# Decay rows on GpSimd's queue, a later convolution of B and C, and pooled-mixing weights split two groups at a time

## The chip, the cores and the metric

The kernel runs on one core of one Trainium2 chip. The time is device microseconds of one launch, from the first instruction to the last, and the time of a kernel is the median of its runs. Engines are named as the profile names them: PE is TensorE (matmuls; PEld its loads of weights), DVE is VectorE, ACT ScalarE, POOL GpSimd and SP SyncE. SyncE does no arithmetic here, it issues transfers. A transfer (DMA) stands in the queue of the engine that issues it, and an engine that waits before an issue holds back all issues behind it.

## The reference, cut to what matters

One layer of a hybrid trunk for 512 tokens of width 1024, in float32. A normed and modulated input `h` goes through one large projection, whose columns are split over three mixers that work beside each other. Their outputs are projected, gated and summed; an MLP follows.

```python
z, xbc, dt_raw, q, k, v, u, gates = jnp.split(h @ w_in, splits, axis=-1)

xbc = silu(causal_dwconv(xbc, conv_w, conv_b))          # 4 taps, 1536 channels
xs, Bm, Cm = jnp.split(xbc, [1024, 1280], axis=-1)      # x; B and C: 2 groups x 128 each
dt = softplus(dt_raw + dt_bias)                         # 16 heads
# _ssd, chunks of 128 tokens:
X = xc * dt
a_cum = cumsum(dt * A)                                  # within a chunk
decay = exp(where(causal, a_cum[l] - a_cum[s], -inf))   # per head, 128 x 128
y_diag = ((C @ B^T) * decay) @ X
y_off = (C @ prev) * exp(a_cum)                         # prev: states carried over chunks
y = y_diag + y_off + D * xc;  y = rms(y * silu(z)) * ssd_norm_w;  y_ssd = y @ w_ssd_out

# three groups of dilated attention, 4 heads of 128 each, mixed by their log-sum-exp
y_attn = sum_g(softmax_g(lse) * out_g) @ w_attn_out

# pooling: windows 2, 4, 8, 16, one per group of 256 channels
pooled = window_mean(u_g) - u_g
y_pool = (concat_g(pooled_g @ w_pool_mix[g]) * pool_scale) @ w_pool_out

x = x + g1 * ((g_ssd * y_ssd + g_attn * y_attn + g_pool * y_pool) @ w_out)
x = x + g2 * (square(relu(h2 @ w_ff1)) @ w_ff2)         # h2: normed again, modulated
```

The modulation (shifts, scales and the gates g1, g2) is `silu(c) @ w_ada + b_ada`.

## The kernel before, in words

Everything lies transposed in SBUF, 128 channels on the partitions by 512 tokens, in blocks of that size; `blk` hands out 49 blocks in turn, `psm` and `acc` the 8 PSUM banks. A block that is handed out again is written only when its last reader is done; a load into it waits for that reader.

A float32 product is made of three products of halves: a weight tile `raw` (512 KB, 128x1024, issued on SP, L287) is split by ScalarE into a high part `wh` (cast, L279) and by VectorE into the rest `wl` (subtraction, L280), and `mm3` (L294, L295, L296) multiplies low by high, high by high, high by low. There are four buffers for `raw` and three pairs for the halves. `gemm_feat` makes four banks `psacc` of 512 tokens at once; `evac` copies them out. The modulation that is not yet needed is worked out along the way: `ada_load` (L240, two loads `wa` of 256 KB on SP) and `ada_dot` (L246, a product with a sum on VectorE, then `modv`), one such job at every second weight tile.

The program text is one long list of gemms; `tick()` is called after each weight tile and runs the next job of the list `side`, so that scores, convolutions, the state-space steps and the pooling lie between the matmuls of a gemm. Within the text a scheduler of the framework sets each engine's order by priority: loads and splits of weights are drawn ahead (AHEAD), evacuations too (SOON), the rest stands where it is written.

The stretch that the change touches runs from the values of the attention to the gates of the state-space branch:

- `attn_out` (L715 to L738), as side jobs of the gemm of B and C: TensorE sums one head's output in the bank `pso`, ScalarE copies it (L736), VectorE subtracts (L737).
- `conv_silu` (L846 to L852) for one tile of 128 channels: ScalarE scales (L848), VectorE adds three shifted taps (L850), ScalarE takes the silu (L852). It is called for B and C (four tiles, L1083) and for x (four tiles per group).
- `ssd_states`: the transposes of B, the product of B and C (`pscb`, L869; masked into `cb`, L870), then per chunk the transposes of x (`psX`), `X` (VectorE, L882), `Xd` (L887), the states `psst` (L891) and the carried states `prev` (first by ScalarE, L895, then by VectorE).
- `ssd_heads`: two heads at a time. The cumulated decay of each head stands as one row of 512 numbers in `prow`, a small tensor in DRAM. For each of the 16 heads one transfer spreads its row over 128 partitions into a block `M` (256 KB, L912, on SP). Then `e` (exp, ScalarE, L917), the differences (VectorE L924 for one head of a pair, ScalarE L922 for the other), the exp (ScalarE, L925), the product with `cb` (VectorE, L926), and the matmuls `psy` with `X` (L932).
- `project` (L751 multiplies by the gate `sg`), first for the attention.
- `pool` (windows by doubling shifted sums, VectorE) and `pool_mix` (L989 on): per group of channels a weight `wmix` of 128x512 is loaded (L991) and split by `wsplit`, in the same buffers as streamed weights, just ahead of its 12 matmuls into two banks `psmix`.

ScalarE keeps one table of functions at a time; a change from copies and exps to silu and back shows in the profile as `ACT_TABLE_LOAD`.

Of the kernel before, what the change touches and what calls it, by code (L numbers as in the profile page):

```python
# [10 lines left out]
F32 = mybir.dt.float32  # L11
F32R = mybir.dt.float32r
AF = mybir.ActivationFunctionType
ALU = mybir.AluOpType
# [3 lines left out]
P = 128  # L18
D = 1024
T = 512  # L20
# [78 lines left out]
def kernel(ctx: ExitStack, tc: tile.TileContext, a: dict, out: bass.AP, dbg=None):  # L99
    nc = tc.nc  # L100
# [3 lines left out]
    raws = ctx.enter_context(tc.tile_pool(name="raws", bufs=4))  # L104
    wsp = ctx.enter_context(tc.tile_pool(name="wsp", bufs=3))
    exp = ctx.enter_context(tc.tile_pool(name="exp", bufs=1))
# [6 lines left out]
    def uid(s):  # L113
        cnt[0] += 1
        return f"{s}_{cnt[0]}"

    class Slots:
# [12 lines left out]
        def free(self, t):  # L130
            self.idle.append(self.used.pop(id(t))[0])
# [3 lines left out]
    def blk(name, dt=F32):  # L135
        return sb.take(name, dt)
# [7 lines left out]
    def doubles(name, tags=("L0", "L1", "N0", "N1")):  # L144

        ts = [exp.tile([P, 2, T], F32R, tag=tag, name=uid(name)) for tag in tags]
        return [t[:, i, :] for t in ts for i in range(2)]

    def small(shape, name, bufs=1, dt=F32):
        return sm.tile(shape, dt, tag=name, name=uid(name), bufs=bufs)  # L150

    def psm(name="m"):
        return banks.take("ps" + name, F32)
# [9 lines left out]
    V, S = nc.vector, nc.scalar  # L163
# [112 lines left out]
    def wsplit(raw, shape):  # L276
        wh = wsp.tile(shape, F32R, tag="wh", name=uid("wh"))
        wl = wsp.tile(shape, F32R, tag="wl", name=uid("wl"))
        S.copy(wh, raw)  # L279
        V.tensor_tensor(wl, raw, wh.bitcast(F32), ALU.subtract)  # L280
        return wh, wl
# [59 lines left out]
    with tc.manual_schedule(engines={E.DVE, E.Activation, E.PE, E.SP}):  # L341
# [107 lines left out]
        var, rt, r, t = (small([P, 4], "rx" + n) for n in "vryt")  # L449
# [266 lines left out]
    def attn_out(h, pTs, vals):  # L716
        hs = slice(h * P, (h + 1) * P)
        op = psm("o")
        ov = op.rearrange("p (j r) -> p r j", r=4)
        for gi in range(3):  # L720
            pT, vs = pTs[gi], vals[gi]
            for b in range(4):
                if gi == 0:
                    od = op[:, b * P : (b + 1) * P]
                    for kb in range(max(0, b - 1), b + 1):
                        cs = (b % 2) * 2 * P + (kb - b + 1) * P
                        mm(od, lhsT=vs[kb][:, hs], rhs=pT[b // 2][:, cs : cs + P], start=(b == 0), stop=False, skip_group_check=True)  # L727
                else:
                    mm(ov[:, b, :], lhsT=vs[b][:, hs], rhs=pT[0][:, b * P : (b + 1) * P], start=False, stop=(gi == 2 and b == 3), skip_group_check=True)  # L729
            free(*pT)  # L730
        if h == 0:
            places = doubles("o")
            oh.extend(places[:4])
            ol.extend(places[4:])
        with tc.high_priority(offset=SOON):
            S.copy(oh[h], op)  # L736
            V.tensor_tensor(ol[h], op, oh[h].bitcast(F32), ALU.subtract)  # L737
        free(op)  # L738


# [29 lines left out]
    st = {}  # L770
# [75 lines left out]
    def conv_silu(x, n):  # L846
        t = blk("conv")
        S.activation(t, x, AF.Identity, bias=vc("conv_b", n), scale=cw[:, 3, n : n + 1])  # L848
        for i in range(1, 4):
            V.scalar_tensor_tensor(t[:, i:], x[:, : T - i], cw[:, 3 - i, n : n + 1], t[:, i:], ALU.mult, ALU.add)  # L850
        free(x)
        S.activation(t, t, AF.Silu)  # L852
        return t

    hp = lambda t: t.rearrange("p (h e) -> p h e", h=8)

    def ssd_states(g, xs, BC):

        BT, CT = BC[g], BC[2 + g]
        Bt, cb = blk("Bt"), blk("cb")  # L860
# [43 lines left out]
    def ssd_heads(g, j, xs, z):  # L904

        X, prev, cb, CT = st[g]
        pc, npc, prow = st["pc"], st["npc"], st["prow"]

        Ms = [blk("M") for _ in range(2)]
        for half in range(2):  # L910
            hd = g * 8 + 2 * j + half
            nc.sync.dma_start(Ms[half], prow[hd : hd + 1, :].broadcast_to([P, T]))  # L912
        yield
        e = blk("e")
        for half in range(2):
            hd, M, fs = g * 8 + 2 * j + half, Ms[half], slice(64 * half, 64 * half + 64)
            S.activation(e[fs, P:], M[fs, P:], AF.Exp, scale=-1.0)  # L917
            for c in range(4):
                cs = slice(c * P, (c + 1) * P)
                hc = slice(c * 16 + hd, c * 16 + hd + 1)  # L920
                if half:
                    S.activation(M[:, cs], M[:, cs], AF.Relu, bias=npc[:, hc])  # L922
                else:
                    V.tensor_scalar(M[:, cs], M[:, cs], pc[:, hc], 0.0, ALU.subtract, ALU.max)  # L924
            S.activation(M, M, AF.Exp, scale=-1.0)  # L925
            V.tensor_tensor(M, M, cb, ALU.mult)  # L926
        yield
        yp = psm("y")
        for c in range(4):
            cs = slice(c * P, (c + 1) * P)  # L930
            for half in range(2):
                mm(yp[half * 64 : half * 64 + 64, cs], lhsT=X[c][:, (2 * j + half) * 64 : (2 * j + half + 1) * 64], rhs=Ms[half][:, cs], start=True, stop=True)  # L932
        free(*Ms)
        y = xs[j]
        V.scalar_tensor_tensor(y, xs[j], dcol[:, 4 * g + j : 4 * g + j + 1], yp, ALU.mult, ALU.add)
        free(yp)
        op = psm("yo")
        for c in range(3):
            cs = slice((c + 1) * P, (c + 2) * P)
            mm(op[:, cs], lhsT=prev[c][:, j * P : (j + 1) * P], rhs=CT[:, cs], start=True, stop=True)  # L940
        V.tensor_tensor(e[:, P:], op[:, P:], e[:, P:], ALU.mult)
        free(op)
        V.tensor_tensor(y[:, P:], y[:, P:], e[:, P:], ALU.add)
        show(f"y{g}{j}", y)
        free(e)
        V.tensor_tensor(y, y, z[j], ALU.mult)
        free(z[j])
        if j == 3:
            free(*X, *prev, cb, CT)
        st["sums", g] = add_square(st.get(("sums", g)), y)  # L950
# [17 lines left out]
    def pool(half):  # L968
        us = evac(gemm_feat(w_in, 8, U + half, hh, hl), "u")
        for j in range(4):  # L970
            gi = 2 * half + j // 2
            u = us[j]
            cur, d = u, 1
            while d < WINDOWS[gi]:
                nx = blk("win")
                V.tensor_copy(nx[:, :d], cur[:, :d])
                V.tensor_tensor(nx[:, d:], cur[:, d:], cur[:, : T - d], ALU.add)
                if cur is not u:
                    free(cur)
                cur, d = nx, 2 * d  # L980
            V.tensor_tensor(cur[:, : d - 1], cur[:, : d - 1], C("edge")[:, gi * 16 : gi * 16 + d - 1], ALU.mult)
            V.scalar_tensor_tensor(cur, cur, 1.0 / d, u, ALU.mult, ALU.subtract)
            free(u)
            x, y = split(cur, "pd")
            free(cur)
            dh.append(x)
            dl.append(y)

    def pool_mix(gi):  # L989
        raw = raws.tile([P, 2, 256], F32, tag="raw", name=uid("wmix"))  # L990
        nc.sync.dma_start(raw, a["w_pool_mix"][gi])  # L991
        wh, wl = wsplit(raw, [P, 2, 256])
        for m in range(2):
            ps = psm("mix")
            cs = slice(m * P, (m + 1) * P)
            for k in range(2):
                mm3(ps, wh[:, k, cs], wl[:, k, cs], dh[2 * gi + k], dl[2 * gi + k], k == 0, k == 1)
            x, y = blk("poolh", F32R), blk("pooll", F32R)
            S.activation(x, ps, AF.Copy, scale=vc("pool_scale", gi * 2 + m))
            V.scalar_tensor_tensor(y, ps, vc("pool_scale", gi * 2 + m), x.bitcast(F32), ALU.mult, ALU.subtract)  # L1000
            free(ps)
            ph_.append(x)
            pl_.append(y)
        free(*dh[2 * gi : 2 * gi + 2], *dl[2 * gi : 2 * gi + 2])
# [12 lines left out]
    def call(f, *args):  # L1017
        side.append(lambda: f(*args))

    probs, vals, stats, pTs, oh, ol = [], [], [], [], [], []  # L1020
# [59 lines left out]
    for h in range(4):  # L1080
        call(out_head, h)
    ps = evac(gemm_feat(w_in, 8, BCC, hh, hl), "xc")
    BC = [conv_silu(ps[i], 8 + i) for i in range(4)]  # L1083
    xs0 = take_x(0)
    rest(1)
    do(ssd_states(0, xs0, BC), 6)
    z0 = take_z(0)
    do_heads(0, xs0, z0)
    xs1 = take_x(1)
    z1 = take_z(1)  # L1090
    do(ssd_states(1, xs1, BC), 6)
    sg = gate(GA, 0)
# [3 lines left out]
    project(a["w_attn_out"], 4, 1, oh, ol, sg, first=True)  # L1096
    show("oT", [h.bitcast(F32) for h in oh + ol])
    for half in range(2):
        pool(half)
        rest(2)  # L1100
        call(pool_mix, 2 * half)
        call(pool_mix, 2 * half + 1)
# [50 lines left out]
    with tc.manual_schedule(engines={E.DVE, E.Activation, E.PE}):  # L1153
# [64 lines left out]
        ps = out_block(tb, 0)  # L1218
        r = scale(sum_tokens(ta, sq))
        residual(tb, 0, ps)  # L1220
        ps = out_block(tb, 1)
# [262 lines left out]
```

## Time and profile before

| | us |
|---|---|
| three runs | 1097.83, 1096.16, 1095.39 |
| median | 1096.16 |
| the profiled execution | 1098.25 |
| its span | 1096.5 |
| PE busy | 1087.1 (99%) |
| DVE busy | 717.4 (65%) |
| ACT busy | 527.8 (48%) |
| POOL busy | 3.6 (0%) |
| six loads on GpSimd's queue (`al` four times, `toNat`, `toMod`) | 256 KB each |
| 16 loads of decay rows on SP's queue | 256 KB each |

The clock of TensorE was granted in full throughout (1.00). In the profile a time is counted from the start of the span, and a row of a timeline shows the start, the duration, the engine, the line, the operation, the tile written and the tiles read, and in brackets how long the engine sat idle before it and what released it. "psacc<-hl,wh" is a matmul that reads `hl` and `wh` and writes the bank `psacc`. A busy share near 100% of TensorE says that it nearly always had work, and the few stalls are found one by one, in the waits and in the starts of neighbouring matmuls. An idle time of VectorE or ScalarE matters only where TensorE then waits.

### The profile page before, as it was taken

What the parts mean: (1) busy time and instruction counts of PE and PEld (TensorE: products, weight loads), DVE (VectorE), ACT (ScalarE), POOL (GpSimd) and SP (SyncE); (2) the same over time, 40 slices, a digit from 0 to 9 for tenths busy, and PEclk for the clock granted to TensorE, in tenths of its full rate; (3) what the DMA queues carried; (4) which work ended last, traced back from release to release, by engine and by line L of the source; (5) the groups of instructions that cost most, each with busy time, mean ns of one, the idle gap of its engine ahead of it and who ended that gap; (6) DMA issues with size and microseconds to landing.
All of it is one profiled execution on the core that took longest, in us unless ns stands there. A gap on an engine that the chain in (4) does not pass through costs nothing.

```text
span 1096.5 us, 14976 instructions
## 1 busy us (share of the span) xinstructions
PE 1087.1 (99%) x5806; PEld 927.0 (85%) x5806; DVE 717.4 (65%) x1383; ACT 527.8 (48%) x845; POOL 3.6 (0%) x10
## 2 busy tenths in 40 slices
PE   9999999999999999999999999999999999999998
PEld 7878888888887877888888888899889989989987
DVE  8975874582776778568843424577787587686664
ACT  8965875543695536625432123354344334335330
POOL 0000000000000000000000000000000000000000
PEclk9999999999999999999999999999999999999999
DMA  9853342443542354321232325360214224134032
GB/s 349 306 183 98 128 134 86 152 168 102 173 125 87 117 181 136 104 97 58 96 115 97 106 96 163 97 230 1 79 57 154 65 90 136 59 114 135 20 116 77
DMA packets 46666, 133.98 MB, mean 122 GB/s; under 512 B 5362, under 2 KB 6130, under 8 KB 46596
## 3 DMA queue, kind: packets, MB, share of 16 engines
q1 hardware_dynamic: 45392, 130.28, 36.0%
q0 software_dynamic: 480, 1.57, 0.5%
q10 hardware_dynamic: 724, 1.18, 0.3%
q8 instruction: 45, 0.74, 0.3%
q14 instruction: 25, 0.20, 0.1%
HBM read 130.89 MB, written 2.13 MB: 121 GB/s over the span
## 4 chain that ended last, share of the span: by engine, by line
PE 87%; ACT 4%; DVE 3%; DMA 3%; issue 1%; SPq 0%; ACTq 0%; DVEq 0%
PE psacc L294 22%; PE psacc L296 22%; PE psacc L295 22%; PE psacc L1345 11%; PE psacc L534 4%; DMA M<-prow 2%; PE psS L613 1%; DMA wa<-in_w_ada_dram 1%; DVE conv L850 1%; ACT wh L279 1%; PE pso L729 1%; PE pso L727 1%; DVE wl L280 1%; PE pskT L597 0%; PE psqT L592 0%
## 5 line engine op out<-in xcount | busy, mean ns | idle before, releaser
L280 DVE TENSOR_TENSOR wl<-raw,wh 128x1024 fp32r<-128x1024 f32 x140 | 171.0, 1222 | 192.2 <-ACT wh L279 190.9
L279 ACT CAST wh<-raw 128x1024 fp32r<-128x1024 f32 x140 | 146.8, 1050 | 241.1 <-PE psacc L295 168.8
L294 PE MATMUL psacc<-hl,wh 128*128 128x512 f32 x416 | 166.6, 401 | 3.4 <-DVE X L882 2.2
L295 PE MATMUL psacc<-hh,wh 128*128 128x512 f32 x416 | 162.1, 390 | 0.0
L296 PE MATMUL psacc<-hh,wl 128*128 128x512 f32 x416 | 162.0, 390 | 0.0
L295 PE MATMUL psacc<-ah,wh 128*128 128x512 f32 (+1 forms) x260 | 100.4, 386 | 0.0
L294 PE MATMUL psacc<-al,wh 128*128 128x512 f32 (+1 forms) x260 | 100.4, 386 | 0.0
L296 PE MATMUL psacc<-ah,wl 128*128 128x512 f32 (+1 forms) x260 | 100.3, 386 | 0.0
L294 PEld LDWEIGHTS psacc<-hl,wh 128*128 128x128 f32 x416 | 78.2, 188 | 21.7 <-DVE X L882 2.7
L295 PEld LDWEIGHTS psacc<-hh,wh 128*128 128x128 f32 x416 | 78.2, 188 | 16.9 <-issue 1.4
L296 PEld LDWEIGHTS psacc<-hh,wl 128*128 128x128 f32 x416 | 78.1, 188 | 16.7
L294 PE MATMUL psacc<-wl,rh 128*128 128x512 f32 x192 | 76.9, 401 | 0.0
L296 PE MATMUL psacc<-wh,rl 128*128 128x512 f32 x192 | 75.5, 393 | 0.0
L295 PE MATMUL psacc<-wh,rh 128*128 128x512 f32 x192 | 75.3, 392 | 0.0
L296 PEld LDWEIGHTS psacc<-ah,wl 128*128 128x128 f32 x260 | 48.8, 188 | 9.9
L294 PEld LDWEIGHTS psacc<-al,wh 128*128 128x128 f32 x260 | 48.9, 188 | 9.7
L295 PEld LDWEIGHTS psacc<-ah,wh 128*128 128x128 f32 x260 | 48.9, 188 | 9.6
L1405 DVE SCALAR_TENSOR_TENSOR xr<-psacc,modv,xr 128x512 f32<-128x512 f32 (+1 forms) x65 | 44.7, 739 | 18.6 <-PE psacc L296 18.6
L246 DVE SCALAR_TENSOR_TENSOR wa<-wa,crow 128x512 f32<-128x512 f32 x64 | 43.1, 688 | 20.0 <-DMA wa<-in_w_ada_dram 20.0
L296 PEld LDWEIGHTS psacc<-wh,rl 128*128 128x128 f32 x192 | 36.0, 188 | 7.6
L294 PEld LDWEIGHTS psacc<-wl,rh 128*128 128x128 f32 x192 | 36.1, 188 | 7.3 <-ACT qT L593 0.2
L295 PEld LDWEIGHTS psacc<-wh,rh 128*128 128x128 f32 x192 | 36.1, 188 | 7.0
(408 smaller groups left out, 2360.8 us busy)
## 6 DMA issues: line engine op xcount, KB each, us to landing
raw<-in_w_in_dram SPq DMA_DIRECT2D x80, 512.0 KB, 3.5
raw<-in_w_ff_dram SPq DMA_DIRECT2D x52, 512.0 KB, 3.7
wa<-in_w_ada_dram SPq DMA_DIRECT2D x64, 256.0 KB, 3.6
wada<-in_w_ada_dram SPq DMA_DIRECT2D x14, 512.0 KB, 7.8
rawl<-in_w_ff_dram SPq DMA_DIRECT2D x12, 512.0 KB, 3.5
wst<-in_w_in_dram SPq DMA_DIRECT2D x16, 256.0 KB, 7.8
M<-prow SPq DMA_DIRECT2D x16, 256.0 KB, 3.8
raw<-in_w_ssd_out_dram SPq DMA_DIRECT2D x8, 512.0 KB, 3.5
```

What stands on the lines that cost most here:

```text
L246: V.scalar_tensor_tensor(wa[i], wa[i], 1.0, crow[i], ALU.mult, ALU.mult, accum_out=d[:, i : i + 1])
L279: S.copy(wh, raw)
L280: V.tensor_tensor(wl, raw, wh.bitcast(F32), ALU.subtract)
L294: mm(ps, lhsT=wh, rhs=xl, start=first, stop=False)
L295: mm(ps, lhsT=wh, rhs=xh, start=False, stop=False)
L296: mm(ps, lhsT=wl, rhs=xh, start=False, stop=last)
L534: mm(ps[j], lhsT=t[:, j, :], rhs=w, start=first, stop=last)
L613: mm(so[b], lhsT=qT[:, b * P : (b + 1) * P], rhs=kT[:, (b + 1) * P - n : (b + 1) * P], start=True, stop=True)
L727: mm(od, lhsT=vs[kb][:, hs], rhs=pT[b // 2][:, cs : cs + P], start=(b == 0), stop=False, skip_group_check=True)
L729: mm(ov[:, b, :], lhsT=vs[b][:, hs], rhs=pT[0][:, b * P : (b + 1) * P], start=False, stop=(gi == 2 and b == 3), skip_group_check=True)
L1345: mm(o, lhsT=x[:, cs], rhs=y, start=first and k == 0 and j == 0 and n == 0, stop=k == 3 and n == 2, skip_group_check=True)
L1405: V.scalar_tensor_tensor(xT[d][:, ts], p[:, : ts.stop - ts.start], modv[:, 3, d : d + 1], xT[d][:, ts], ALU.mult, ALU.add)
```

## The change

It has three parts.

1. The 16 transfers of decay rows are issued by GpSimd, on its own queue, in place of SP.
2. The four convolutions of B and C are held behind the two instructions that take the last head's attention output out of its bank (`issue_after` on the copy and the subtraction, kept in `st["edges"]`).
3. The weights of pooled mixing are loaded and split by a new side job, `mix_weights`, once for two groups: two loads into one `raw` buffer, one cast and one subtraction of 128x1024 into tiles of their own (the pool `exp`, whose tags L0, N0, L1 and N1 hold the attention output until its projection is done). The job is called ahead of `pool` of that half; `pool_mix` takes the halves from a list.

```diff
@@ attn_out
         with tc.high_priority(offset=SOON):
-            S.copy(oh[h], op)
-            V.tensor_tensor(ol[h], op, oh[h].bitcast(F32), ALU.subtract)
+            st["edges"] = S.copy(oh[h], op), V.tensor_tensor(ol[h], op, oh[h].bitcast(F32), ALU.subtract)
         free(op)
@@ ssd_heads
-            nc.sync.dma_start(Ms[half], prow[hd : hd + 1, :].broadcast_to([P, T]))
+            nc.gpsimd.dma_start(Ms[half], prow[hd : hd + 1, :].broadcast_to([P, T]))
@@ before pool_mix
+    mixw = []
+
+    def mix_weights(n):
+
+        raw = raws.tile([P, 2, T], F32, tag="raw", name=uid("wmix"))
+        for i in range(2):
+            nc.sync.dma_start(raw[:, i, :].rearrange("p (k c) -> p k c", k=2), a["w_pool_mix"][2 * n + i])
+        wh, wl = (exp.tile([P, 2, T], F32R, tag=f"{x}{n}", name=uid("wm" + x)) for x in "LN")
+        S.copy(wh, raw)
+        V.tensor_tensor(wl, raw, wh.bitcast(F32), ALU.subtract)
+        mixw.extend([t[:, i, :].rearrange("p (k c) -> p k c", k=2) for t in (wh, wl)] for i in range(2))
+
     def pool_mix(gi):
-        raw = raws.tile([P, 2, 256], F32, tag="raw", name=uid("wmix"))
-        nc.sync.dma_start(raw, a["w_pool_mix"][gi])
-        wh, wl = wsplit(raw, [P, 2, 256])
+        wh, wl = mixw[gi]
@@ main sequence
     ps = evac(gemm_feat(w_in, 8, BCC, hh, hl), "xc")
-    BC = [conv_silu(ps[i], 8 + i) for i in range(4)]
+    with tc.issue_after(st["edges"][0].ins), tc.issue_after(st["edges"][1].ins):
+        BC = [conv_silu(ps[i], 8 + i) for i in range(4)]
     xs0 = take_x(0)
@@
     for half in range(2):
+        call(mix_weights, half)
         pool(half)
         rest(2)
         call(pool_mix, 2 * half)
```

All lines of the kernel from L738 to L988 stand one line earlier after the change (X is L881, the decay row's transfer L911).

The scheduler's order changes with it. VectorE, around the end of the first half of the attention's projection (`sg` is the gate, `X` the first chunk of the second group, each `M` one decay row, `wa` a load of the modulation), before:

```order
L870 TENSOR_TENSOR cb_818_3957<-pscb_820_3964,cst_78 128x512
L924 TENSOR_SCALAR M_877_4245<-M_877_4245,pc_216_947 128x128
L926 TENSOR_TENSOR M_904_4413<-M_904_4413,cb_818_3957 128x512
L924 TENSOR_SCALAR M_882_4279<-M_882_4279,pc_216_947 128x128
L924 TENSOR_SCALAR M_877_4245<-M_877_4245,pc_216_947 128x128 x2
L751 TENSOR_TENSOR sg_806_3914<-psacc_810_3922,sg_806_3914 128x512
L751 TENSOR_TENSOR sg_807_3915<-psacc_811_3923,sg_807_3915 128x512
L751 TENSOR_TENSOR sg_808_3916<-psacc_812_3924,sg_808_3916 128x512
L751 TENSOR_TENSOR sg_809_3917<-psacc_813_3925,sg_809_3917 128x512
L882 TENSOR_TENSOR X_825_4005<-psX_824_4000,dt_205_885 128x512
```

and now:

```order
L869 TENSOR_TENSOR cb_818_3957<-pscb_820_3964,cst_78 128x512
L923 TENSOR_SCALAR M_877_4245<-M_877_4245,pc_216_947 128x128
L925 TENSOR_TENSOR M_904_4413<-M_904_4413,cb_818_3957 128x512
L246 SCALAR_TENSOR_TENSOR wa_885_4298,dot_887_4302<-wa_885_4298,crow_3_81 128x512
L923 TENSOR_SCALAR M_882_4279<-M_882_4279,pc_216_947 128x128
L248 TENSOR_TENSOR modv_16_94<-dot_887_4302 128x1
L923 TENSOR_SCALAR M_877_4245<-M_877_4245,pc_216_947 128x128
L750 TENSOR_TENSOR sg_806_3914<-psacc_810_3922,sg_806_3914 128x512
L750 TENSOR_TENSOR sg_807_3915<-psacc_811_3923,sg_807_3915 128x512
L750 TENSOR_TENSOR sg_808_3916<-psacc_812_3924,sg_808_3916 128x512
L750 TENSOR_TENSOR sg_809_3917<-psacc_813_3925,sg_809_3917 128x512
L881 TENSOR_TENSOR X_825_4005<-psX_824_4000,dt_205_885 128x512
```

A product of the modulation and its sum have come in front of the third row's M, and one of the two later Ms has gone behind X. SP's queue at the same place, before:

```order
L287 DMA raw_874_4215<-in_w_attn_out_dram 128x1024
L912 DMA M_877_4245<-prow_1036 128x512
L912 DMA M_878_4246<-prow_1036 128x512
L912 DMA M_882_4279<-prow_1036 128x512
L240 DMA wa_885_4298<-in_w_ada_dram 128x512
L287 DMA raw_879_4249<-in_w_attn_out_dram 128x1024
L287 DMA raw_892_4315<-in_w_in_dram 128x1024
```

and now:

```order
L287 DMA raw_874_4215<-in_w_attn_out_dram 128x1024
L240 DMA wa_885_4298<-in_w_ada_dram 128x512
L287 DMA raw_879_4249<-in_w_attn_out_dram 128x1024
L240 DMA wa_911_4453<-in_w_ada_dram 128x512
L287 DMA raw_892_4315<-in_w_in_dram 128x1024
```

The three rows are gone from it; they stand in the same order on GpSimd's queue, which holds nothing else from the first row on. ScalarE, from the copies of B and C on (`xc` are the four banks, `conv_604` to `conv_607` their convolutions, `pso` the last head), before:

```order
L331 COPY xc_600_2825<-psacc_570_2607 128x512
L848 ACTIVATE conv_604_2833<-xc_600_2825,vec_1_79 128x512
L331 COPY xc_601_2826<-psacc_571_2608 128x512
...
L852 ACT_TABLE_LOAD
L852 ACTIVATE conv_604_2833<-conv_604_2833 128x512
L736 CAST o_579_2658<-pso_596_2798 128x512
L848 ACTIVATE conv_605_2839<-xc_601_2826,vec_1_79 128x512
L848 ACTIVATE conv_606_2845<-xc_602_2827,vec_1_79 128x512
L848 ACTIVATE conv_607_2851<-xc_603_2828,vec_1_79 128x512
L917 ACT_TABLE_LOAD
L917 ACTIVATE e_726_3459<-M_704_3376 64x384
```

and now:

```order
L736 CAST o_579_2658<-pso_596_2798 128x512
L847 ACTIVATE conv_604_2833<-xc_600_2825,vec_1_79 128x512
L847 ACTIVATE conv_605_2839<-xc_601_2826,vec_1_79 128x512
L847 ACTIVATE conv_606_2845<-xc_602_2827,vec_1_79 128x512
L847 ACTIVATE conv_607_2851<-xc_603_2828,vec_1_79 128x512
L916 ACTIVATE e_726_3459<-M_704_3376 64x384
L916 ACTIVATE e_726_3459<-M_705_3377 64x384
L921 ACTIVATE M_705_3377<-M_705_3377,npc_217_948 128x128 x4
L279 CAST wh_625_2962<-raw_624_2960 128x1024
L851 ACT_TABLE_LOAD
L851 ACTIVATE conv_604_2833<-conv_604_2833 128x512
```

The four scalings stand together behind the last head's copy, and the first silu has gone behind the exps `e` of the first two rows.

## The prediction

> **What bounds the kernel now.** I read the page's busy table first, then TensorE's waits, then the timelines around each wait. The busy table (busy us, share of the span, instructions) and the waits (engine, line, releaser: total us, times, longest) say:
>
> ```profile
> PE 1087.1 (99%) x5806; PEld 927.0 (85%) x5806; DVE 717.4 (65%) x1383; ACT 527.8 (48%) x845; POOL 3.6 (0%) x10
> PE psacc L294 <- DVE X L882: 2.2, 1, 2.2
> PE psacc L294 <- DVE conv L935: 0.5, 1, 0.5
> PE psacc L294 <- ACT prev L895: 0.5, 1, 0.5
> ```
>
> TensorE is 99% busy and the change leaves its matmuls as they are; only a stall of it can be won or made. One is large. TensorE's timeline there, and VectorE's and SyncE's ahead of it (start, us, instruction, idle before it and its releaser):
>
> ```profile
> 428.39 0.40 PE L296 MATMUL psacc<-hh,wl 128*128 128x512 f32 x1
> 431.01 0.50 PE L294 MATMUL psacc<-hl,wh 128*128 128x512 f32 x1 [2.22 <-DVE X L882]
> 418.21 2.50 DVE L322 TENSOR_TENSOR ynl<-conv,ynh 128x512 fp32r<-128x512 f32 x4
> 422.34 0.68 DVE L870 TENSOR_TENSOR cb<-pscb,cst 128x512 f32<-128x512 f32 x1
> 423.48 0.29 DVE L924 TENSOR_SCALAR M<-M,pc 128x128 f32<-128x128 f32 x1 [0.45 <-DMA M<-prow]
> 423.68 0.69 DVE L926 TENSOR_TENSOR M<-M,cb 128x512 f32<-128x512 f32 x1
> 427.29 0.68 DVE L924 TENSOR_SCALAR M<-M,pc 128x128 f32<-128x128 f32 x3 [2.92 <-DMA M<-prow]
> 427.88 2.48 DVE L751 TENSOR_TENSOR sg<-psacc,sg 128x512 f32<-128x512 f32 x4
> 430.27 0.68 DVE L882 TENSOR_TENSOR X<-psX,dt 128x512 f32<-128x512 f32 x1
> 417.48 0.33 SPq L287 DMA_DIRECT2D raw<-in_w_attn_out_dram  x1
> 419.53 2.20 SPq L912 DMA_DIRECT2D M<-prow  x3
> 421.83 0.37 SPq L240 DMA_DIRECT2D wa<-in_w_ada_dram  x1
> ```
>
> Three decay rows are issued from 419.53, each into a block that one of VectorE's ynl has just freed. The first lands in time for the M at 423.48. The third holds VectorE for 2.92 us, until 427.29; behind it stand sg and X, and TensorE waits for X's bank. Matmuls here otherwise start 0.23 us apart, so the stall costs 431.01 − 428.39 − 0.23 = 2.39 us. The other stall on the path of a decay row is earlier:
>
> ```profile
> 311.42 0.33 SPq L912 DMA_DIRECT2D M<-prow  x1
> 314.81 0.29 DVE L924 TENSOR_SCALAR M<-M,pc 128x128 f32<-128x128 f32 x1 [2.32 <-DMA M<-prow]
> 319.62 1.28 ACT L852 ACT_TABLE_LOAD   x1 [1.36 <-DVE conv L850]
> 336.15 0.60 ACT L895 COPY prev<-psst 128x512 f32<-128x512 f32 x1
> 335.92 0.39 PE L296 MATMUL psacc<-hh,wl 128*128 128x512 f32 x1
> 336.81 0.50 PE L294 MATMUL psacc<-hl,wh 128*128 128x512 f32 x1 [0.50 <-ACT prev L895]
> ```
>
> A row issued at 311.42 releases VectorE at 314.81, behind it wait the convolutions of x, behind those ScalarE, whose copy prev ends late: TensorE loses 336.81 − 335.92 − 0.23 = 0.66 us. A third, again behind a row, is at 412:
>
> ```profile
> 412.09 0.39 PE L296 MATMUL psacc<-hh,wl 128*128 128x512 f32 x1
> 412.59 0.71 PE L222 MATMUL psrr<-diag,ones 128*128 128x128 f32 x4
> 406.99 0.28 DVE L924 TENSOR_SCALAR M<-M,pc 128x128 f32<-128x128 f32 x1 [0.89 <-DMA M<-prow]
> ```
>
> That is 412.59 − 412.09 − 0.23 = 0.27 us. The conv stall (L935) follows an adaLN load that the change leaves where it is. So 2.39 + 0.66 + 0.27 = 3.3 us is all that faster rows can bring.
>
> **The change, part by part.** *Rows on GpSimd's queue.* What such a transfer takes, by queue, from the table of issues (KB, median us from issue to landing) and the views of the tiles M, then al:
>
> ```profile
> M<-prow SPq DMA_DIRECT2D x16, 256.0 KB, 3.8
> al<-in_const_dram POOLq DMA_DIRECT2D x4, 256.0 KB, 3.3
> toMod<-in_const_dram POOLq DMA_DIRECT2D x1, 256.0 KB, 4.3
> DMA to landing us min/median/max: 3.1/3.8/6.5
> DMA to landing us min/median/max: 2.9/3.3/4.7
> L178 POOL DMA_DIRECT2D al<-in_const_dram x4: 538/538/672, 53.6 to 147.3; - x4
> ```
>
> Six transfers of the same size on GpSimd's queue took 2.9 to 4.7 us, issue 0.54 to 0.67; on SyncE's 16 rows took 3.1 to 6.5. Their source differs (constants once each, a row of DRAM spread over 128 partitions), so these are bounds, not the price. The three rows wait for the same ynl as before, so GpSimd starts them at 419.5, 420.1 and 420.7 too. What it needs: by the changed order VectorE does cb, M, M times cb, one adaLN dot that stood behind X, the third row's M, one more M, four sg, X. From the first M that is 0.2 + 0.6 + 0.7 + 0.2 + 0.1 + 0.2 + 2.4 + 0.7 = 5.1 us (starts of the quoted rows; the dot as the sg, 0.6, and its sum 0.1). TensorE wants X at 428.39 + 0.23 = 428.62, so the first M may start at 423.5, its row land at 423.4, the third at 425.0. At 3.3 us the rows land at 422.8 and 424.0: no stall. At 4.7 they land at 424.2 and 425.4: 0.8 us of stall are left. At 6.5, as SyncE's third row, the third lands at 427.2, where it did: 0.0 to 0.2 us are won. The dot is new in front of X, and its load is no longer behind the three rows on SyncE: it waits for the product of B and C, which frees its block at 419.72 + 1.05 = 420.8, and lands, by the 3.6 us of its like, at 424.4; VectorE comes to it at 423.5 + 0.2 + 0.6 = 424.3:
>
> ```profile
> 419.72 1.05 PE L869 MATMUL pscb<-conv,conv 128*128 128x128 f32 x8
> wa<-in_w_ada_dram SPq DMA_DIRECT2D x64, 256.0 KB, 3.6
> ```
>
> I take the al rows, which lie nearest to 3.3, and 0.1 of stall for the dot: −2.3 us.
>
> For the row of 311.42 the landing took 3.30 us; at 2.9 the stall at 336 shrinks by 0.4, at 4.7 it grows by 1.4, one for one, since VectorE and ScalarE run without a gap from it to prev. At 3.3: 0. The row before 406.99 had been issued at 402.66 and took 4.31; at 2.9 all 0.27 go, at 4.7 0.4 are added. Between them: 0. Weights on SyncE gain nothing by the rows' absence: they wait for their buffers.
>
> ```profile
> SPq L287 <- DVE wl L280: 436.3, 103, 11.1
> 402.66 4.31 DMA M<-prow
> ```
>
> A rule of the Trainium skill speaks against this part. "SBUF — State Buffer", the box on the "DVE blocks DMA" trap, says that GpSimd writes the descriptors of its transfers itself and is shut out while VectorE runs a copy or tensor_scalar in its two-port mode: 3.1 us in place of 0.62. Six such waits on the three paths would more than eat the gain. The trace has GpSimd issuing in 0.54 and 0.67 us, the second beside busy VectorE; it does not show one beside tensor_scalar, which is short here (0.29).
>
> *B and C behind the last attention output.* ScalarE then does the convolution's four scalings, the exps and the silus in fewer turns: around 290 its table is loaded four times where it was six, 2 × 1.28 = 2.6 us less. Two of the six:
>
> ```profile
> 290.58 1.28 ACT L917 ACT_TABLE_LOAD   x1
> 295.64 1.28 ACT L852 ACT_TABLE_LOAD   x1
> ```
>
> TensorE's waits name nothing of this stretch up to the 336 stall, and the copies of x that ScalarE makes next are of what TensorE has just finished, so what it saves ends as idle time. If it did not, 0.66 could be won at prev; if the scalings, now behind the last copy, came late for the product of B and C, a table load, 1.28, could be lost. I take 0.
>
> *Weights of pooled mixing.* Four subtractions of 0.69 become two of 1.22 (the mean of the streamed weights, which have twice the columns), ahead: −0.3 us on VectorE. The groups of the view of wmix (ns min/median/max) and of the page, and the window in which they lie (us, then busy PE, PEld, DVE, ACT):
>
> ```profile
> L280 DVE TENSOR_TENSOR wl<-wmix,wh x4: 682/691/693, 530.4 to 541.5; 128x512 fp32r<-128x512 f32 x4
> L280 DVE TENSOR_TENSOR wl<-raw,wh 128x1024 fp32r<-128x1024 f32 x140 | 171.0, 1222 | 192.2 <-ACT wh L279 190.9
> 520.00:540.00 20.00, 20.00 (x90) 16.49 (x89) 19.73 (x46) 7.80 (x13) 0.00 (x0) 1.00 0.21 69
> ```
>
> TensorE is busy all 20 us: nothing to win. The cover is thin, VectorE being busy 19.73 of the 20; a second subtraction of 1.22 us ahead of what TensorE waits for there would cost up to 1.2. Both stand, by the order, ahead of the groups that use them, and the streamed weights no longer have small ones between them: 0.
>
> Sum: −2.3 + 0 + 0 + 0. The profiled execution took 1098.25 us (span 1096.5, 1.75 around it), 2.09 above the median of the runs, 1096.16. It gives 1095.95; from the median, 1093.86.
>
> **Rivals.** *B, rows quicker throughout:* 2.9 us each, the least of al. Then 0.4 more go at 336 and 0.27 at 412: 1093.2. For it: the rows no longer queue behind weights. Against: toMod took 4.3. *C, no stall to win:* the third row is late for a reason that the queue does not share (all three read small rows of one tensor, and transfers of weights go on beside them), or the runs that were timed do not have the late landing: the profiled one is 2.09 above their median, about the stall's own size. Then −0.2 at most: 1096.0. *D, the rows land later on GpSimd's queue:* its issue waits for VectorE's tensor_scalars, or the spread row costs there what it did here over the median, 6.5 − 3.8 = 2.7, on top of 4.7. The third row lands at 420.7 + 7.4 = 428.1, +0.9; the row of 311.42 at 4.7 adds 1.4, that of 402.66 0.4: +2.7, 1098.9. It decides from a landing over 3.3 us at 311 and over 6.5 at 420.7. *The change does not do what it says* is excluded by its order: all 16 rows stand on GpSimd's queue.
>
> **How the numbers follow.** Forecast A 0.45, B 0.13, C 0.26, D 0.16. A measurement tells 0.2%, 2.2 us, from no change: the bounds are 1093.97 and 1098.35. A sits on the lower one: its own range is 1093.5 (0.1 and 0.27 more) to 1094.8 (0.8 of the stall left and 0.1 for the dot), so of its 0.45 about 0.27 are faster and 0.18 within. B is faster; C is within; D gives 0.15 slower and 0.01 within. Faster 0.40, same 0.45, slower 0.15. The range leaves out the upper part of D (0.12) and little below B (0.03), and holds C with the spread of its runs: 1092.2 to 1097.8.
>
> **What would show it.** Right: rows on GpSimd's queue landing in 3 to 4 us; no wait of TensorE for X L881 near 428; VectorE idle under 1 us between 423 and 430; four table loads from 284 to 305; stalls at 336 and 412 as they are; none from 500 to 560. Wrong: the third row after 425.4, an adaLN dot waiting over 1 us for its load there, GpSimd's issues over 1 us, or a new wait of TensorE behind a row.

## The result and the profile after

The change makes the kernel slower by 0.7%: 1104.01 us median of 6 runs (1103.15 to 1104.52) against 1096.18 before (1094.87 to 1098.60), a ratio of 1.0067, 95% interval 1.0054 to 1.0080. The forecast was 1093.9, in a range of 1092.2 to 1097.8. The profiled execution took 1103.29 us (span 1101.2, clock 1.00).

TensorE's waits in the changed kernel (engine, line, releaser: total us, times, longest), and below them those of a second profile of the kernel before, which took 1095.0 us (span 1093.2) and is nearer to its median than the first. Three short waits that are the same in both are left out:

```profile
PE psacc L294 <- DVE X L881: 2.1, 2, 1.8
PE psrr L222 <- DVE diag L221: 1.5, 1, 1.5
PE pssx L412 <- DVE sq L421: 1.5, 1, 1.5
PE psacc L294 <- ACT prev L894: 1.5, 1, 1.5
PE psst L890 <- DVE Xd L886: 0.9, 1, 0.9
PE psacc L294 <- DVE conv L958: 0.4, 1, 0.4
PE psacc L294 <- DVE conv L934: 0.3, 1, 0.3
```

```profile
PE pssx L412 <- DVE sq L421: 0.4, 1, 0.4
PE psacc L294 <- DVE conv L935: 0.4, 1, 0.4
PE psacc L294 <- ACT prev L895: 0.2, 1, 0.2
```

Six waits are new or grown. In starts of matmuls, over the usual 0.23 us, they are 1.46 us at 334 and 337 (Xd, X), 1.66 at 340 (prev), 1.70 at 417 (diag), 0.46 at 423 (conv L958) and 2.02 at 436 (X); conv L934 takes 0.46 where it took 0.55. The sixth is that of the start (sq), before any row is loaded. Its 1.1 us are not lost in full, since the matmul before it starts earlier: by 315 the same matmul starts only 0.30 us later than in the second profile of before. From there on it starts 3.4 us later at 342, 5.8 at 431 and 7.8 at 438, and the spans differ by 8.0. So nearly all of the loss lies in three places, from 333 to 340, from 412 to 423 and at 436, and the long waits there lie behind decay rows. The 0.46 at 423 does not: VectorE has one split of a weight further ahead in its order there, and the same wait stands in runs below in which no row is late at 412.

The rows themselves, by the view of the tile M:

```profile
L911 POOL DMA_DIRECT2D M<-prow x16: 536/536/538, 244.0 to 454.4; - x16
  DMA M<-prow: 24.1, 12
DMA to landing us min/median/max: 3.3/4.3/8.1
```

The median landing went from 3.8 to 4.3 us, the longest from 6.5 to 8.1; of the 16 rows of the kernel before the trace tells 12 landings, and that of the second row at 288 is not among them. The first chain, from the timelines (start, us, instruction, idle before it and its releaser), answers to the rows of 311 to 337 in the prediction:

```profile
293.72 0.53 ACT L916 ACTIVATE e<-M 64x384 f32<-64x384 f32 x1 [2.43 <-DMA M<-prow]
295.94 0.52 ACT L916 ACTIVATE e<-M 64x384 f32<-64x384 f32 x1 [1.70 <-DMA M<-prow]
309.31 0.58 ACT L331 COPY xc<-psacc 128x512 f32<-128x512 f32 x1
310.77 2.33 DVE L849 SCALAR_TENSOR_TENSOR conv<-xc,vec,conv 128x511 f32<-128x511 f32 x3
313.62 0.54 POOL L911 DMA_DIRECT2D M<-prow  x1 [25.28 <-ACT xc L331]
317.92 0.29 DVE L923 TENSOR_SCALAR M<-M,pc 128x128 f32<-128x128 f32 x1 [3.68 <-DMA M<-prow]
339.23 0.60 ACT L894 COPY prev<-psst 128x512 f32<-128x512 f32 x1
339.88 0.50 PE L294 MATMUL psacc<-hl,wh 128*128 128x512 f32 x1 [1.49 <-ACT prev L894]
```

ScalarE waits for two rows in turn, ahead of the silus, and comes to the copies of x at 309.31 (307.58 before). The next row waits for a convolution that ends at 310.77 + 2.33 = 313.10 and for the last copy of x, which ends at 313.13; it is issued 0.49 us after that, at 313.62, and takes 4.20 us, where it had been issued at 311.42, 0.02 after its release, and taken 3.3. VectorE's M starts at 317.92 in place of 314.81, 3.1 us later, and prev at 339.23 in place of 336.15, again 3.1. TensorE itself was 0.3 us later at 321 (start-up); the other 2.8 are what the stalls from 333 to 340 add to those of before.

The second chain ends at 417. Its row is released at 405.91, issued 0.53 us later, at 406.44, and lands at 411.25, after 4.81 us (4.31 before); ScalarE has stood idle for it and VectorE's diag comes late:

```profile
411.32 1.28 ACT L916 ACT_TABLE_LOAD   x1 [6.91 <-DMA M<-prow]
416.87 0.71 PE L222 MATMUL psrr<-diag,ones 128*128 128x128 f32 x4 [1.54 <-DVE diag L221]
```

The third is the place of the forecast gain:

```profile
424.56 1.74 POOL L911 DMA_DIRECT2D M<-prow  x3 [17.59 <-DVE ynl L322]
425.75 0.33 SPq L240 DMA_DIRECT2D wa<-in_w_ada_dram  x1
431.36 0.69 DVE L246 SCALAR_TENSOR_TENSOR wa<-wa,crow 128x512 f32<-128x512 f32 x1 [2.09 <-DMA wa<-in_w_ada_dram]
431.98 0.29 DVE L923 TENSOR_SCALAR M<-M,pc 128x128 f32<-128x128 f32 x1
435.58 0.50 PE L294 MATMUL psacc<-hl,wh 128*128 128x512 f32 x1 [1.85 <-DVE X L881]
```

The adaLN load, now ahead on SyncE's queue, is issued among the three rows and takes 5.6 us; the third row takes 6.19 (425.76 to 431.96). VectorE meets both at the same moment, so this profile does not tell which of the two alone would have cost how much.

### The profile page after: what moved, and what is told of

The parts are those of the page before. It is cut to its first block, busy times and chain, and to the rows that moved or that the text cites. A ratio compares the mean times of both kernels' runs of the same rounds, so it can differ in the third digit from the quotient of the medians.

```text
span 1101.2 us, 14958 instructions
## 1 busy us (share of the span) xinstructions
PE 1087.6 (99%) x5806; PEld 926.7 (84%) x5806; DVE 716.5 (65%) x1381; ACT 524.9 (48%) x841; POOL 12.1 (1%) x26
## 4 chain that ended last, share of the span: by engine, by line
PE 63%; DVE 3%; ACT 3%; DMA 2%; issue 1%; SPq 0%; ACTq 0%; POOLq 0%; DVEq 0%
PE psacc L294 16%; PE psacc L295 16%; PE psacc L296 16%; PE psacc L1356 11%; DMA wa<-in_w_ada_dram 2%; DVE conv L849 1%; DMA M<-prow 1%; ACT wh L279 1%; DVE wl L280 1%; PE psst L890 0%; PE psy L931 0%; PE psmix L296 0%; PE psmix L295 0%; PE psmix L294 0%; DVE wa L246 0%
```

## Experiments

Two theories at first. **The queue**: a row comes later from GpSimd's queue, and TensorE pays where a chain through a row has no slack. **The order**: the edge on the convolutions puts the exps of two rows ahead of ScalarE's silus. All ratios below are to runs of the kernel before on the same chip; 0.2% is about what a measurement can tell.

**The three parts apart.** One part of the diff alone, and the change without its first part.

```diff
# rows alone                       # edge alone: issue_after(...) around BC
-nc.sync.dma_start(Ms[half], ...)  # mix alone:  mix_weights, mixw
+nc.gpsimd.dma_start(Ms[half], ...) # undo rows: edge and mix, rows on nc.sync
```

Rows alone. 

> Only the first part: the 16 decay rows on GpSimd's queue, all else as before. Theory 1 (the queue): a row comes later from GpSimd's queue, about 0.5 us from its release to its issue in the changed kernel's trace where SyncE took about 0.06, and a median landing of 4.3 us where it was 3.8; so this part alone carries most of the loss, +4 to +8 us (1100 to 1104). Theory 2 (the order): the loss comes from the exps of two rows that stand ahead of ScalarE's silus, put there by the edge on the convolutions; then this part alone costs +0 to +2 (1096 to 1098).

Measured: 1102.58 us, ratio 1.0060 (1.0048 to 1.0072), +6.8 us, as theory 1 has it. But the order moved here too, without the edge: ScalarE takes the exp of the second row ahead of its next silus (at 295.10, after 1.80 us of waiting). So this run alone does not part the theories. TensorE's longer waits in it:

```profile
PE psacc L294 <- ACT prev L895: 1.5, 1, 1.5
PE psrr L222 <- DVE diag L221: 1.4, 1, 1.4
PE psacc L294 <- DVE X L882: 1.4, 1, 1.4
PE psacc L294 <- ACT pT L711: 1.0, 1, 1.0
```

Edge alone. 

> Only the second part: the convolutions of B and C behind the last attention output, rows on SyncE, weights of pooled mixing as before. Theory 1: within 1 us of before (1095 to 1097). Theory 2: both exps ahead of the silus wait for their rows on ScalarE, which comes to the copies of x about 1.4 us late as in the changed kernel; every later row follows: +2 to +5 us (1098 to 1101).

Measured: 1096.16, ratio 1.0003 (0.9994 to 1.0011). No loss, though both exps stand ahead of the silus: theory 2 fails as the cause of the loss. But the edge is not without effect: on SyncE's queue the second of the two exps waits 0.48 us where it waited 1.70 above, and the copy of x stands at 308.01 (309.31 above). In the profile TensorE loses 1.45 us at 336 and only 0.23 at 429. The rows of ScalarE's timeline with the edge alone, and TensorE's at 336:

```profile
293.64 0.53 ACT L916 ACTIVATE e<-M 64x384 f32<-64x384 f32 x1 [2.53 <-DMA M<-prow]
294.64 0.52 ACT L916 ACTIVATE e<-M 64x384 f32<-64x384 f32 x1 [0.48 <-DMA M<-prow]
337.71 0.50 PE L294 MATMUL psacc<-hl,wh 128*128 128x512 f32 x1 [1.28 <-ACT prev L894]
```

Mixing alone. 

> Only the third part: weights of pooled mixing split ahead. Both theories: no stall of TensorE between 480 and 560, within 1 us of before (1095 to 1097). A third theory, that the split costs where VectorE has no room, would give +1 to +3 and a wait of TensorE in that stretch.

Measured: 1097.30, ratio 1.0013 (1.0004 to 1.0022), with a wide scatter (1095.15 to 1099.85). The third theory has something to it. In the profiled execution, the slowest of them, TensorE loses 1.33 us at 497 (another 2.6 of its 4.9 us over the second profile of before had been lost by 252, ahead of anything that this part changes). VectorE does the split, a weight and parts of the pooling ahead of the evacuation of psy, and TensorE waits for that, by the two engines' timelines:

```profile
487.74 1.23 DVE L998 TENSOR_TENSOR wmN<-wmix,wmL 128x1024 fp32r<-128x1024 f32 x1 [0.46 <-ACT wmL L997]
498.51 0.50 PE L294 MATMUL psacc<-hl,wh 128*128 128x512 f32 x1 [1.17 <-DVE conv L935]
```

In the profile of the whole change this stall is absent. What makes the times scatter stays open.

Rows undone. 

> The change with its first part undone: edge and pooled mixing changed, the rows on SyncE. Theory 1: the loss is gone, 1095 to 1097. Theory 2: the loss stays to more than half, 1099 to 1102.

Measured: 1096.75, ratio 1.0012 (1.0004 to 1.0021). Theory 1 again, with the edge's order left in: the loss is gone but for about 1 us. Rows 6.8 and the other two parts 1.0 make up the 7.8 of the change.

**The premise, and what in the queue it is.** The kernel before was profiled once more, and the rows were put on a third queue and cut in two.

```diff
# ScalarE's queue
+nc.scalar.dma_start(Ms[half], prow[hd : hd + 1, :].broadcast_to([P, T]))
# halves
+for r in (0, 64):
+    nc.gpsimd.dma_start(Ms[half][r : r + 64], prow[hd : hd + 1, :].broadcast_to([64, T]))
```

Before again. 

> The kernel before, profiled a second time: is the stall of 2.39 us at 428, on which the forecast rested, part of every execution? If it is: TensorE waits 2 to 3 us for X L882 again and the third row takes 6 us or more. If it belonged to that one execution: the third row lands in 4 to 5.5 us, the wait is under 1 us, and the time is 1095 to 1096.5.

Measured: 1095.0. The third row (issued at 419.80) lands after 4.21 us, VectorE waits 0.35 for it, and no wait of TensorE for X is listed. VectorE's timeline of this second profile, and SyncE's:

```profile
417.27 2.50 DVE L322 TENSOR_TENSOR ynl<-conv,ynh 128x512 fp32r<-128x512 f32 x4
418.59 1.53 SPq L912 DMA_DIRECT2D M<-prow  x3
424.04 0.68 DVE L924 TENSOR_SCALAR M<-M,pc 128x128 f32<-128x128 f32 x3 [0.35 <-DMA M<-prow]
```

The stall of 2.39 us did not come back; how many of the timed runs have it is not known. With rows on SyncE the third row landed after 4.36 and 4.14 us in the profiles with the edge, and after 5.1 in that of mixing, where TensorE lost 0.95 us to X.

Rows from ScalarE. 

> The kernel before with the 16 rows issued from ScalarE's queue in place of SyncE's: another queue than the weights', as on GpSimd, but one whose transfers no engine has to write. If GpSimd's own work is what makes a row late, the first packet follows the issue after about 0.95 us as on SyncE (1.24 to 2.4 on GpSimd) and rows land after 3.1 to 4 us. If sharing the transfer engines with the weights of another queue does it, the rows at 288 and at 420 take 5.5 to 8 us as on GpSimd. The time itself is not decisive, since ScalarE also stands still where a row waits for its block: 1096 to 1104.

Measured: 1096.79, ratio 1.0005 (0.9996 to 1.0015): nothing lost, though ScalarE also stands in its queue. The second row at 288 took 7.28 us here too, and the third at 419.8 took 5.05, so long landings beside the weights are not GpSimd's alone; yet in quiet places rows land after 2.98 to 3.17 us. A second queue as such is not the cause. The run is no clean comparison of queues, though, since the order moved with it. The row of 311 is issued later still and lands at 318.2, 1.8 us after that of the rows alone, and costs nothing: VectorE has put its M behind the convolutions.

```profile
314.88 0.33 ACTq L912 DMA_DIRECT2D M<-prow  x1
314.15 2.78 DVE L850 SCALAR_TENSOR_TENSOR conv<-xc,vec,conv 128x511 f32<-128x511 f32 x4 [1.61 <-ACT conv L848]
```

Halves. 

> Rows on GpSimd's queue, each as two transfers of 64 partitions: the same bytes, twice as many issues, all else as with the first part alone (1102.6). If GpSimd's work per transfer makes the rows late, the second half is issued about 0.6 us after the first, each chain through a row gets that much longer, and the time grows by 1 to 3 us, to 1103.5 to 1106. If the bytes on the shared engines make them late: within 1 us of 1102.6.

Measured: 1099.63, ratio 1.0032 (1.0022 to 1.0043): +3.5 us over before where whole rows cost 6.8, which neither side had expected. The second half is issued 0.51 us after the first, and a quiet pair lands 3.6 us after its first issue, as a whole row does. Two other things had changed. The scheduler put VectorE's M of the 311 row behind the convolutions (VectorE's timeline with halves, its last row ScalarE's at 407):

```profile
315.79 2.78 DVE L850 SCALAR_TENSOR_TENSOR conv<-xc,vec,conv 128x511 f32<-128x511 f32 x4 [1.61 <-ACT conv L848]
321.60 0.36 DVE L925 TENSOR_SCALAR M<-M,pc 128x128 f32<-128x128 f32 x1
406.97 1.28 ACT L918 ACT_TABLE_LOAD   x1 [4.92 <-DMA M<-prow]
```

And e reads 64 partitions only, so that ScalarE goes on at 406.97, as the first half of that row lands, while the second comes at 409.4. The test does not isolate the issue's price, since order and waits moved with it. It agrees with the cost of a row lying in what stands behind it.

**Which rows.** Three rows alone on GpSimd's queue, or all but these.

```diff
+q = nc.gpsimd if (g, j, half) in ((0, 1, 1), (0, 2, 0), (1, 3, 0)) else nc.sync   # reverse: not in
+q.dma_start(Ms[half], prow[hd : hd + 1, :].broadcast_to([P, T]))
```

> Only three of the 16 rows on GpSimd's queue, the ones of which the first part's profile shows a stall of TensorE at the end of their chain: the second row at 244 (stall at 251), the row at 311 (stall at 336), the row at 402 (stall at 412); ScalarE's and VectorE's orders stay those of before but for one instruction. If late arrival on these chains is what costs: +2.5 to +4.5 us over before (1098.5 to 1100.5), with stalls near 1.1, 1.7 and 1.6 us. If the loss is in proportion to what goes through GpSimd's queue, or lies in the weights that share the engines: 3/16 of 6.8, +1.3 us or less.

Measured: 1099.66, ratio 1.0033 (1.0021 to 1.0046), +3.6 us: three of sixteen rows bring half of the loss, with ScalarE's exps and silus and VectorE's M in the order of before. Two of the three chains show it, as foreseen in size (1.68 at 336, 1.90 at 413); that of 244 does not (0.23 at 252, as before). TensorE's waits with the three rows, those of the start left out:

```profile
PE psrr L222 <- DVE diag L221: 1.7, 1, 1.7
PE psacc L294 <- ACT prev L895: 1.5, 1, 1.5
PE psacc L294 <- DVE X L882: 0.5, 1, 0.5
PE psacc L294 <- DVE conv L960: 0.4, 1, 0.4
PE psacc L294 <- ACT pT L711: 0.2, 1, 0.2
```

> The reverse: 13 rows on GpSimd's queue, those three on SyncE; orders of ScalarE and VectorE as with all rows on GpSimd. Late arrival on the three chains: +1.5 to +3.5 us left over before (1097.5 to 1099.5), by the rows at 288 and the three at 420. Loss in proportion: 13/16 of 6.8, +5.5 us (1101.5).

Measured: 1097.53, ratio 1.0018 (1.0009 to 1.0027). Thirteen rows on GpSimd's queue cost about 2 us (1.0 to 3.0 by the interval), as late arrival on the three chains had it and not in proportion, and the stalls at 336 and 412 are gone, though both exps stand ahead of the silus here as well. What is left is mainly X at 428 (2053 − 227 ns = 1.83 us), behind the three rows of 420, of which the third took 5.97 us. TensorE's waits with the thirteen:

```profile
PE psacc L294 <- DVE X L882: 1.7, 1, 1.7
PE psacc L294 <- DVE conv L960: 0.4, 1, 0.4
PE psacc L294 <- DVE conv L936: 0.4, 1, 0.4
```

**Earlier issue.** Each pair of rows one step of the heads earlier.

```diff
-        side.append(lambda: next(gens[0]))
+        side.append(lambda: (next(gens[0]), next(gens[1])))
-                for i in (j + 2, j + 1, j):
+                for i in (j + 3, j + 1, j):
```

On SyncE. 

> The kernel before with each pair of rows issued one step of the state-space heads earlier, still on SyncE: two pairs at about 288, none on the path at 311. If the arrival of the row issued at 311 sets the stall at 336, that stall is gone (0.66 us) and VectorE no longer waits 2.3 us at 314; 1094.5 to 1096. If something else sets it, no change or, by the two pairs landing together ahead of the weights at 288, a loss of 1 us.

Measured: 1095.18, ratio 0.9986 (0.9978 to 0.9995). TensorE loses 0.2 us at 336.

On GpSimd. 

> All 16 rows on GpSimd's queue, each pair one step earlier as in the run that did this on SyncE: no row on the path at 311. If lateness on the path costs, the stall at 336 shrinks below 0.7 us and the time lies 1 to 3 us under that of all rows on GpSimd: 1099.5 to 1101.5. If what costs is what GpSimd's transfers do to the weights, no gain: 1102 to 1104.

Measured: 1096.23, ratio 1.0005 (0.9996 to 1.0014): about 6 us less than rows on GpSimd's queue in the old places, and less than either side had expected. The rows are no quicker; they are asked for while there is time. The view of M, VectorE's timeline at 313, and TensorE's wait for prev:

```profile
L912 POOL DMA_DIRECT2D M<-prow x16: 536/536/538, 245.1 to 440.4; - x16
DMA to landing us min/median/max: 3.6/4.1/8.4
312.96 4.77 DVE L850 SCALAR_TENSOR_TENSOR conv<-xc,vec,conv 128x511 f32<-128x511 f32 x7 [0.33 <-ACT conv L848]
PE psacc L294 <- ACT prev L895: 0.5, 1, 0.5
```

VectorE runs its convolutions at 313 without a row in front of them. So most of the loss is late arrival on chains without slack, not what GpSimd's transfers do to others: the same 16 transfers stand in the same queue here. Something is left, since the earlier rows on SyncE's queue, with VectorE's convolutions in the same order at 313, had a ratio of 0.9986, about 2 us less; TensorE loses 0.66 us at 336 and 0.40 at 412 here, 0.2 and nothing there.

Both. 

> A version meant to beat both: rows on SyncE one step earlier, and B and C behind the last attention output. The first alone gave 1095.18 and the second alone nothing; if the second's stall at 336 (1.4 us there) was a row's lateness it is gone too, and the time is 1094.5 to 1095.3; if it comes from both exps standing ahead of the silus, 1095.5 to 1096.5.

Measured: 1094.90, ratio 0.9993 (0.9984 to 1.0002); the stall at 336 is 0.23 us, as expected if with the edge alone it had been a row's lateness. It is the lowest median of all, but its interval does not exclude no change; the earlier rows alone have one below 1, by 0.14%, which is less than the 0.2% that a measurement can tell. Either beats the changed kernel by some 9 us.

## Why the prediction was wrong, step by step

Two steps failed. The one gain in the sum, −2.3 us, was taken from a stall that the median run cannot be shown to have; and the paths behind the rows of 311 and 402 were put at 0, by a landing of 3.3 us and nothing else. In the changed kernel the three chains cost TensorE some 7 us more than in the second profile of before.

- **The term of −2.3 us rested on one execution.** The stall at 428 was real there, but it is absent in the second profile of before. The profiled run's 2.09 us above the median was the sign; the prediction put it under rival C and still took the 2.3 off the median. In the second profile there was nothing to win.
- **The landing was taken from the wrong rows.** 3.3 us is right for a quiet place (3.26 to 3.58 in several rows). At 288, 311 and 420, where SyncE has weights or adaLN loads under way, rows took 3.7 to 8.1. The trace before showed such landings on SyncE's own queue: 6.13 us at 288, and 3.85, 3.87 and 6.53 at 420. The six transfers of al and its like were bounds for a quiet queue only.
- **"GpSimd starts them at 419.5, 420.1 and 420.7 too" failed.** The same ynl, with rows alone:

```profile
421.09 2.49 DVE L322 TENSOR_TENSOR ynl<-conv,ynh 128x512 fp32r<-128x512 f32 x4
422.67 1.74 POOL L912 DMA_DIRECT2D M<-prow  x3 [17.38 <-DVE ynl L322]
```

  The issue follows the start of the four subtractions after 1.58 us where SyncE's (418.59 − 417.27) followed after 1.32; the second subtraction ends 1.29 after that start. So 0.29 us in place of 0.03, and 0.49 at 313 and 0.53 at 406 in the changed kernel. No part of the sum had this term.
- **The row of 311: the mechanism was right, the sum short.** One for one was right. The bound of +1.4 counted the landing alone (it grew by 0.9); the later issue, 2.2 us, came on top, 1.7 of it from ScalarE's later copies of x and 0.5 from release to issue.
- **B and C: "it ends as idle time" failed on GpSimd's queue.** Tables were counted and two were saved. But the new order, which stood in the rows shown, has both exps ahead of the first silu, and with GpSimd's landings ScalarE waits 2.43 and 1.70 us there: the stalls from 333 to 340 come to 3.1 us, against 1.68 with the rows alone, though by the times the edge and the mixing together cost 1.0 us with the rows on either queue. On SyncE's queue the step's zero holds in the time (+0.3, interval over no change), though not in the stall at 336.
- **Pooled mixing: 0 was nearly right.** Alone it costs about 1.4 us, near the 1.2 given for a lost cover, but at 497, where the first split stands, not between 520 and 540; with the edge, no such stall shows.
- **The adaLN dot in front of X: 0.1 was mis-sized.** It waits 2.09 us, since its load is issued among the three rows and takes 5.6 us, not 3.6; behind the three rows on SyncE's queue the same load had taken 6.05 (421.83 to 427.88 in the first profile of before). The third row lands at the same moment, so the dot's own share is not shown.
- **Rival D had the right mechanism in the main, rows that land later, and the right chains.** Its two reasons, VectorE's tensor_scalars and a price of the spread row, are not shown. Of its points one was passed (4.20 at 311 over 3.3), the other not (6.19 at 420.7 under 6.5). It was priced at +2.7 and came to 7.8, as it left out the issue and ScalarE's order and started from an execution that already had the stall at 428. Its chance of 0.16 was too low: it was known that VectorE and ScalarE run without a gap behind the row of 311, so that any lateness there counts in full, and nothing in the trace showed GpSimd's queue beside busy loads. Of the prediction's signs of being wrong, the dot's wait of over 1 us and new waits behind rows came; GpSimd's issues stayed at 0.54 us.

The rule cited against the change, from the Trainium skill ("SBUF — State Buffer", the box on the "DVE blocks DMA" trap), points the right way, but its mechanism is not shown by these runs: all 16 issues took 0.536 to 0.538 us, whatever VectorE did. Whether VectorE's short tensor_scalars delay the first packet was not isolated: after the issue at 323.16, with two of them under way, it came after 2.10 us, but SyncE had issued loads of 512 and 256 KB within the 1.2 us before.

## What to carry to other kernels

Before a transfer moves to another queue, follow the chain behind its landing to the engine that bounds the kernel: where that chain has no slack, price the time from release to issue, the issue and the landing in that stretch, not in a quiet one. If a row is late, ask for it earlier: that was worth about 6 us on the slower queue and left about 2 between the two queues. Look at the order too: a change of queue moved ScalarE's and VectorE's order, and the same late row costs nothing where nothing stands behind it. A stall that ends in a landing far off its median is a term of a sum only when a second profile shows it.

## What the hardware showed that was not expected

From the packets in the trace, a row on GpSimd's queue sends its first packet at the earliest 1.23 us after its issue, one on SyncE's after 0.95. From release to issue GpSimd mostly took 0.2 to 0.5 us and SyncE 0.02 to 0.03. Together that makes 0.5 to 0.8 us more for most rows, even where nothing else moves. The Trainium skill ("DMA: Bandwidth & Descriptors", "Latency and other measured facts") gives about 1 us and about 0.6 us to the first byte; the step between the two agrees roughly (0.28 here), the time to the issue is not in it.

Beside SyncE's loads the rows of one burst spread out. At 425 the three rows on GpSimd's queue were issued 0.6 us apart and landed at 428.28, 430.64 and 431.96; in the second profile of before, on SyncE's queue, they landed at 422.71, 423.36 and 424.01, and with the earlier issue, on GpSimd's queue but with no adaLN load issued among them, at 422.95, 423.57 and 424.52. So the queue alone does not set it. At 288 the second row took 8.11 us on GpSimd's queue, 7.28 on ScalarE's and, in the run with three rows on GpSimd's, 7.02 on SyncE's: that stretch is slow for every queue. How much of the later landings on GpSimd's queue comes from the queue's own later start and how much from SyncE's loads beside it was not parted.
